# S5 output of a two-block layer: the chunk products moved ahead of the scan, into two open PSUM banks

## The chip, the cores and the metric

The kernel runs on one core of a Trainium2 chip. The metric is the time of one execution in device microseconds; less is better. Before the change it is 1471.91 us (median of three runs, 1470.84 to 1474.93).

## What is computed

The program computes two blocks of a model on 512 tokens of 1024 columns. The first block mixes the tokens by an S5 layer (256 columns) and an SSD layer (768 columns), then adds cross attention and a convolved feed-forward part. The second block has HGRN2 and forgetting attention and a mixture of 16 experts. The change lies in the S5 layer of the first block:

```python
bu_re = jnp.einsum('blgc,gpc->blgp', uf, bb_re)
bu_im = jnp.einsum('blgc,gpc->blgp', uf, bb_im)
...
_, _, h_re, h_im = lax.associative_scan(combine, (a_re, a_im, bu_re, bu_im), axis=1)
y = (jnp.einsum('blgp,gcp->blgc', h_re, c_re.astype(f32))
     - jnp.einsum('blgp,gcp->blgc', h_im, c_im.astype(f32)))
y = y + uf * d_skip.astype(f32).reshape(S5_GROUPS, S5_GROUP_DIM)
y = jax.nn.gelu(y.reshape(bsz, l, S5_WIDTH))
y = y * jax.nn.sigmoid(y @ w_glu.astype(f32))
```

There are 16 groups of 16 columns, each with 64 complex states.

## The kernel before

The kernel cuts the 512 tokens into 64 chunks of 8. Within a chunk the output is a plain matrix product of the chunk's inputs with a Toeplitz block (`s5T`, 128x128 for a group); what comes from earlier chunks is the product of the state before the chunk (`H`, 64 rows for a group, real and imaginary plane) with `s5O`. So the output of a group is one **chunk product** (128 rows, 64 moving columns) plus two **state products** (64 rows, 64 moving columns). Groups come in pairs `gp` of 8; of a pair, the group `g2 = 0` has its states in partitions 0 to 63, and `g2 = 1` in partitions 64 to 127.

`s5_main` (L661 to L765) does the S5 layer in order: the inputs `U` come from DRAM; 32 small products give the chunks' sums `S` (L686), which ScalarE takes from two PSUM banks to SBUF (L688); VectorE scans over chunks (L698 to L713) and forms the state before each chunk, first its real plane, then its imaginary one (L727 to L731); TensorE makes the output (L740 and L742); ScalarE takes it from PSUM (L744, `s_yo`); it goes through DRAM to change its layout (L745, L749), and then come the skip and the GELU (L754, L755), the gate's product (L760), its sigmoid (L762) and the result (L763). All products of this function are in full float32: for each the trace shows two weight loads and two matmuls, so counts in the trace are twice those in the code.

`s5_main` is a generator. It is put on a list of background work (L1048) and advanced a step at a time while the units of the projections are traced: first the projection to the SSD inputs x (128x512 tiles, L1026 to L1036), then that to z (128x260 tiles, L1055). Each unit of a projection is a row of matmuls L276, L277, L278 (three float32r products of a high and a low part) on weights that ScalarE (L270) and VectorE (L271) have split. After z follow the norm of the memory (`mem_norm`; L311, L334, L323, L315), the SSD layer and the projections of the memory to keys and values.

What stands where on each engine is then set by a scheduler: it puts the traced instructions into one in-order queue for each engine, by priority and by when it thinks that their operands are there. PSUM has 8 banks: 4 in the pool `pmm` (`mm`, projections), 2 in `ptr` (`tr`, transposes) and 2 in `psm` (`sm`), which S5 uses. Weights come on the queue of SyncE (SP), into slots that are freed by the splits.

Before the change the output loop opens a bank for `g2 = 0`, makes for each pair the chunk product and the two state products into 64 of its columns, evicts the bank and writes it out, and then does the same for `g2 = 1`:

```python
o = ps[:, gp * 64:gp * 64 + 64]
nc.tensor.matmul(o, s.s5T[:, g].rearrange("p c t -> p (c t)"), U[:, g], start=True, stop=False)
for i in range(2):
    nc.tensor.matmul(o, s.s5O[rows, i, gp].rearrange("p c t -> p (c t)"), H[rows, i, gp],
                     start=False, stop=i == 1)
```

The scheduler draws the first chunk product of each bank far ahead, behind L686.

Of the kernel before, what the change touches and what calls it, by code (L numbers as in the profile page):

```python
# [7 lines left out]
F32 = mybir.dt.float32  # L8
# [10 lines left out]
P = 128  # L19
T = 512  # L20
# [3 lines left out]
SLOT = 4 * 260    # values of a block of weights in a partition  # L24
# [7 lines left out]
CAP = 96          # slots of an expert in one go  # L32
# [8 lines left out]
class Split:  # L41
    """an operand as two float32r parts whose sum is the float32 value"""
# [5 lines left out]
class Back:  # L48
    """pieces of work traced between the units of a projection"""
# [21 lines left out]
class Kern:  # L71
# [11 lines left out]
    @contextmanager  # L83
    def ahead(s, n=3000):
        """what is traced here goes before what is ready with it"""
        tc = s.tc
        p = tc.cur_priority
        tc.cur_priority = p - n
        yield
        tc.cur_priority += n  # L90

# [1 line left out]
    def consts(s):  # L93
# [14 lines left out]
        # -1e30 where the free index is below the partition, and where it is above it  # L108
# [10 lines left out]
    def bcast_pe(s, pool, row, name):  # L119
        """a row of 1024 in all partitions"""  # L120
        t = pool.tile([P, D], F32, name=name)
        for half in range(2):
            cs = slice(half * 512, half * 512 + 512)
            ps = s.pmm.tile([P, 512], F32, name="mm")
            s.nc.tensor.matmul(ps, s.ones[0:1, :], row[:, cs], start=True, stop=True)
            s.nc.scalar.activation(t[:, cs], ps, AF.Copy)
        return t

# [1 line left out]
    def plan_units(s):  # L130
        """blocks of weights in the order in which they are used"""
# [59 lines left out]
        s.plan = []       # engines and fences of the next splits, where not the usual ones  # L191

    def ring(s, kind, of=None):
        """the pools of a ring, one slot of each in turn"""
# [4 lines left out]
    def fill(s, splits=999, most=999):  # L199
        """loads and splits ahead of their use, as far as the slots go"""  # L200
        nr, nh = len(s.rings["raw"]), len(s.rings["hi"])
        while True:
            if s.u_load < len(s.units) and s.raw_live < nr and most:
# [4 lines left out]
                if n == "w_in" and off % ld == 776:   # the last of z, then dt  # L208
# [27 lines left out]
    def wunit(s, n, off, ld, kk, cols, keep=0):  # L236
        """the next block; the blocks taken before the last keep ones are done with"""
# [18 lines left out]
    def later(s, f, k=0):  # L256
        """f is traced when the next block of weights is taken (k: so many later)"""
# [23 lines left out]
    def rstd(s, ss, n, width, pool, v0=None, out=None):  # L281
        """(ss / width + eps) ** -0.5 for [128, n], the power refined by a Newton step;
        v0 in place of eps"""
# [33 lines left out]
    def transposes(s, src, k0, nk, dst, tt, dk=None):  # L317
        """src [128, nk*128] of token tile tt to the k-tiles of dst"""
# [11 lines left out]
    def norm_T(s, x, gain, dst, tt):  # L330
        """rows x [128, 1024] of token tile tt, normalised, scaled; returned: transposed into dst"""
# [15 lines left out]
    def projT(s, src, cols, ld, hT, evac, halves=False):  # L347
        """256 columns from each of cols of src as [column, token] tiles: evac(i, psum)"""
# [29 lines left out]
    def projR(s, src, ld, nk, get, x, after, tail=3, mid=None, lag=2, order=None):  # L378
        """x[:, tt] += (rows of get(k)) @ src, 1024 columns; after(tt) when a token tile is complete:
        it returns what is left to do lag tiles later; mid(tt) when its first half is"""  # L380
# [32 lines left out]
    def softplus_neg(s, pool, ax, shape):  # L413
        """log1p(exp(-|x|)) from |x|"""
# [23 lines left out]
    def s5_params(s, pc, po):  # L438
        """per (pair of groups, state) on partitions: kernels of a chunk of 8 tokens.
        pc: parameter columns pool (short lived), po: results"""  # L440
        nc, A = s.nc, s.A
        V = nc.vector
        cm = s.cols1          # [128, 96] columns
# [30 lines left out]
        # cos and sin of th: whole turns taken off exactly, then the sine in [-pi, pi]  # L474
# [20 lines left out]
        # powers 0..8 of a: [128, re/im, power, gp]  # L495
# [7 lines left out]
        def cpow(dst, src, n1):  # L503
            """dst[n1+1 .. 2 n1] = src[n1] * src[1 .. n1]"""
# [13 lines left out]
        # powers of a^8: [128, re/im, power, gp], negated imaginary part as third plane  # L518
# [7 lines left out]
        # powers 7..0 of a: [re/im, gp, s]  # L526
# [4 lines left out]
        # f = (a - 1) / lambda  # L531
# [17 lines left out]
        # Bb = f * B: [128, re/im, gp, c]  # L549
# [11 lines left out]
        # O = C a^t, t = 0..7, its imaginary part negated: [128, re/im, gp, t, c]  # L561
# [20 lines left out]
        # Bb with each channel 8 times: [128, re/im, gp, (c, s)]  # L582
# [4 lines left out]
        # K[(c', s), g, (t, c)] = Re sum_p C a^t Bb, the same for each s  # L587
# [15 lines left out]
        # shift by s: Toeplitz blocks  # L603
# [11 lines left out]
        # X = a^(7-s) Bb, transposed to [(c, s), re/im, gp, (g2, p)]  # L615
# [25 lines left out]
        # O a: [128, re/im, gp, (c, t)]  # L641
# [6 lines left out]
        # re' = re ar - im ai, -im' = (-im) ar - re ai  # L648
# [12 lines left out]
    def s5_main(s, pe, pu, dr):  # L661
        """u -> gelu, gate; tokens as in s5ud, (token in a chunk, chunk)"""
# [19 lines left out]
        for i in range(2):  # L682
# [6 lines left out]
            yield  # L689
        p8 = s.p8  # L690
# [13 lines left out]
        # what enters each block of 8 chunks  # L704
# [11 lines left out]
        # state before each chunk  # L716
# [16 lines left out]
        yd = dr.tile([256, 512], F32, name="s5_yd")  # L733
        for g2 in range(2):
            rows = slice(g2 * 64, g2 * 64 + 64)
            ps = s.psm.tile([P, 512], F32, name="sm")
            for gp in range(8):
                g = 2 * gp + g2
                o = ps[:, gp * 64:gp * 64 + 64]
                nc.tensor.matmul(o, s.s5T[:, g].rearrange("p c t -> p (c t)"), U[:, g], start=True, stop=False)  # L740
                for i in range(2):
                    nc.tensor.matmul(o, s.s5O[rows, i, gp].rearrange("p c t -> p (c t)"), H[rows, i, gp],  # L742
                                     start=False, stop=i == 1)
            nc.scalar.activation(yo[:, g2].rearrange("p g c -> p (g c)"), ps, AF.Copy)  # L744
            nc.sync.dma_start(dap(yd, g2 * 8192, [[64, P], [16384, 8], [1, 64]]), yo[:, g2])  # L745
            yield
# [21 lines left out]
    def ssd_dt(s, pd, x):  # L768
        """from dt before its softplus, [token, (chunk, head)]"""
# [24 lines left out]
        ex = pd.tile([P, 3, 4, 12], F32, name="ssd_ex")   # exp of: cumulated, total, what is left  # L794
# [5 lines left out]
        # the cumulated values as rows (chunk, head), which a matrix product spreads over the partitions  # L800
# [22 lines left out]
    def ssd_mask_unit(s, pl, c, g):  # L823
        """(C B^T masked with the decay), transposed: [s, head, t]"""
# [17 lines left out]
    def ssd_main(s, pl, zs, mixT):  # L842
        """chunks of 128 tokens; zs: silu(z) in [token, channel]"""
# [3 lines left out]
        for c in range(4):  # L847
# [59 lines left out]
            # gate, norm, transposed  # L907
# [8 lines left out]
    def rows_T(s, pool, specs, name):  # L916
        """rows of 128 values, as columns"""
# [12 lines left out]
    def mixer1(s):  # L930
# [9 lines left out]
        with ExitStack() as xc:  # L940
# [14 lines left out]
            # the table of Square is loaded while x comes  # L955
# [23 lines left out]
        # the last third of z, and dt  # L979
# [11 lines left out]
        # u  # L991
        s.s5T = po.tile([P, 16, 16, 8], F32, name="s5_T")      # rows (c', s), columns (c, t)
# [14 lines left out]
        # B, C, x with their convolution  # L1007
# [42 lines left out]
        # z  # L1050
# [1269 lines left out]
```

## Time and profile before

| | us |
|---|---|
| median of three runs | 1471.91 |
| lowest, highest run | 1470.84, 1474.93 |
| span of the profiled execution, first to last instruction | 1470.4 |
| TensorE matmuls busy | 1418.8 (96%) |
| TensorE weight loads busy | 1146.5 (78%) |
| VectorE busy | 977.9 (67%) |
| ScalarE busy | 776.2 (53%) |
| mean granted TensorE clock | 0.978 of full speed |

The profile gives the span of the profiled execution; it is 0.4 us under the lowest run and 1.5 us under the median. TensorE is busy nearly all the time, and its granted clock is below full speed in a few stretches only. A busy share counts an instruction from its start to its end, so a TensorE that is busy can still be slow: at half its clock, or waiting between small products.

### The profile page before, as it was taken

To read this page: it belongs to the slowest core of one execution; us is meant where nothing else is said; L and a number is where in the kernel's file an instruction comes from. 1 tells how busy PE (TensorE), PEld (TensorE's weight loads), DVE (VectorE), ACT (ScalarE), POOL (GpSimd) and SP (SyncE) were. 2 spreads that over 40 slices of the span, in tenths; PEclk is the share of its full clock that TensorE was granted. 3 is DMA by queue.
4 is the path that set the end of the run, shared out by engine and by line. 5 is a ranking of instruction groups with operands and counts; after the bars stand their busy time and mean duration, and the time that the engine had idled before them with its cause. 6 is when DMAs were issued, how large, how long until landed. Compare 5 with 4: busy or idle time off the path is not lost. (4 is left out here: it accounts for less than half of the span.)

```text
span 1470.4 us, 20178 instructions
## 1 busy us (share of the span) xinstructions
PE 1418.8 (96%) x7467; PEld 1146.5 (78%) x7467; DVE 977.9 (67%) x1772; ACT 776.2 (53%) x1198; POOL 103.8 (7%) x103
## 2 busy tenths in 40 slices
PE   7999999999999999999999999999999599999996
PEld 6887988778788888888888889877887367777774
DVE  5989267665546444434463897676545599999997
ACT  6465264434424333323352696454433388888885
POOL 1000000010000000000000400000101211111111
PEclk9999699999999999999999999999999699999998
DMA  6353223423123333233222423130663899999993
GB/s 191 100 131 116 69 86 101 158 72 101 58 72 101 105 98 99 87 99 101 92 95 86 132 74 101 30 89 30 207 237 137 246 351 363 356 344 347 342 350 127
DMA packets 145934, 223.51 MB, mean 152 GB/s; under 512 B 18467, under 2 KB 71107, under 8 KB 145817
## 3 DMA queue, kind: packets, MB, share of 16 engines
q1 hardware_dynamic: 136852, 200.48, 41.8%
q0 software_dynamic: 3568, 10.34, 2.9%
q10 hardware_dynamic: 5412, 11.37, 2.2%
q8 instruction: 59, 0.97, 0.3%
q14 instruction: 43, 0.34, 0.1%
HBM read 208.41 MB, written 14.95 MB: 152 GB/s over the span
## 5 line engine op out<-in xcount | busy, mean ns | idle before, releaser
L271 DVE TENSOR_TENSOR wlo<-raw,whi 128x1024 fp32r<-128x1024 f32 (+1 forms) x351 | 423.5, 1221 | 236.9 <-ACT whi L270 234.4
L270 ACT ACTIVATE whi<-raw 128x1024 fp32r<-128x1024 f32 (+1 forms) x356 | 372.8, 1057 | 293.1 <-PE mm L277 143.1
L276 PE MATMUL mm<-hT_hi,whi 128*128 128x512 f32 (+1 forms) x768 | 283.3, 369 | 1.9 <-DVE x L403 1.7
L278 PE MATMUL mm<-hT_hi,wlo 128*128 128x512 f32 (+1 forms) x768 | 281.6, 367 | 0.0
L277 PE MATMUL mm<-hT_lo,whi 128*128 128x512 f32 (+1 forms) x768 | 280.8, 366 | 0.0
L276 PE MATMUL mm<-whi,hT_hi 128*128 128x512 f32 (+1 forms) x592 | 220.5, 373 | 1.8 <-ACT hT_hi L315 1.8
L278 PE MATMUL mm<-whi,hT_lo 128*128 128x512 f32 (+1 forms) x592 | 220.2, 372 | 0.0
L277 PE MATMUL mm<-wlo,hT_hi 128*128 128x512 f32 (+1 forms) x592 | 219.0, 370 | 0.0
L278 PEld LDWEIGHTS mm<-hT_hi,wlo 128*128 128x128 f32 x768 | 144.7, 188 | 24.4
L276 PEld LDWEIGHTS mm<-hT_hi,whi 128*128 128x128 f32 x768 | 144.2, 188 | 24.7 <-DVE x L403 1.9
L277 PEld LDWEIGHTS mm<-hT_lo,whi 128*128 128x128 f32 x768 | 144.6, 188 | 23.3
L276 PEld LDWEIGHTS mm<-whi,hT_hi 128*128 128x128 f32 x592 | 113.7, 192 | 20.7 <-ACT hT_hi L315 2.7
L278 PEld LDWEIGHTS mm<-whi,hT_lo 128*128 128x128 f32 x592 | 113.8, 192 | 19.6 <-issue 0.8
L277 PEld LDWEIGHTS mm<-wlo,hT_hi 128*128 128x128 f32 x592 | 113.9, 192 | 18.1 <-issue 0.6
L276 PE MATMUL mm<-whi,ex_xh 128*96 128x512 f32 x256 | 102.8, 402 | 1.3 <-ACT ex_xh L315 0.7
L291 POOL TENSOR_TENSOR rs_r<-rs_v,mhalf 128x1 f32<-128x1 f32 (+2 forms) x42 | 33.3, 797 | 998.8 <-DVE rs_v L289 842.7
L277 PE MATMUL mm<-wlo,ex_xh 128*96 128x512 f32 x256 | 101.5, 397 | 0.0
L278 PE MATMUL mm<-whi,ex_xl 128*96 128x512 f32 x256 | 101.1, 396 | 0.0
L276 PEld LDWEIGHTS mm<-whi,ex_xh 128*96 128x96 f32 x256 | 41.7, 163 | 19.1 <-ACT ex_xh L315 1.2
L278 PEld LDWEIGHTS mm<-whi,ex_xl 128*96 128x96 f32 x256 | 41.6, 162 | 18.0
L277 PEld LDWEIGHTS mm<-wlo,ex_xh 128*96 128x96 f32 x256 | 41.8, 163 | 17.0
L1238 DVE SCALAR_TENSOR_TENSOR cv<-mm,cols,cv 128x511 f32<-128x511 f32 (+1 forms) x44 | 33.0, 749 | 30.0 <-ACT cv L1235 29.2
(568 smaller groups left out, 2087.0 us busy)
## 6 DMA issues: line engine op xcount, KB each, us to landing
raw<-in_w_gate SPq DMA_DIRECT2D x64, 512.0 KB
raw<-in_w_up SPq DMA_DIRECT2D x64, 512.0 KB
raw<-in_w_down SPq DMA_DIRECT2D x64, 512.0 KB
raw<-in_ffn_w_up SPq DMA_DIRECT2D x44, 512.0 KB
raw<-in_w_in SPq DMA_DIRECT2D x40, 512.0 KB
raw<-in_ffn_w_down SPq DMA_DIRECT2D x22, 512.0 KB
raw<-in_w_out SPq DMA_DIRECT2D x16, 512.0 KB
raw<-in_w_in SPq DMA_DIRECT2D x8, 520.0 KB
```

Of the source, the lines that this page charges most:

```text
L270: s.hi_op = s.nc.scalar.activation(hv, v, AF.Copy).ins
L271: eng.tensor_sub(lv, v, hv.bitcast(F32))
L276: mm(ps, a.hi[asl], b.hi[bsl], start=first, stop=False)
L277: mm(ps, a.hi[asl], b.lo[bsl], start=False, stop=False)
L278: mm(ps, a.lo[asl], b.hi[bsl], start=False, stop=last)
L291: s.pow_op = nc.gpsimd.tensor_tensor(r, v, s.mhalf[:, :n], OP.pow).ins
L1238: V.scalar_tensor_tensor(y[:, d:], ps[:, :512 - d], cw[:, w:w + 1], y[:, d:], op0=OP.mult, op1=OP.add)
```

## The change

The sixteen chunk products move ahead of the scan: they are made as soon as `U` is there and ScalarE has emptied the two banks of L686, and both banks stay open with their sums until the end. A bank is started once (`start=gp == 0`); the other columns of a bank are then written for the first time without a start. Behind the scan only the 32 state products are left, in the order pair, plane, half: each is followed by one of the other row half, into the other bank. The two evictions and the two writes to DRAM stand together at the end.

```diff
             nc.scalar.activation(S[:, i].rearrange("p g c -> p (g c)"), ps, AF.Copy)
             yield
+
+        yps = [s.psm.tile([P, 512], F32, name="sm") for _ in range(2)]
+        for gp in range(8):
+            for g2 in range(2):
+                g = 2 * gp + g2
+                nc.tensor.matmul(yps[g2][:, gp * 64:gp * 64 + 64], s.s5T[:, g].rearrange("p c t -> p (c t)"), U[:, g],
+                                 start=gp == 0, stop=False)
+            if gp == 3:
+                yield
+        yield
         p8 = s.p8
...
         yd = dr.tile([256, 512], F32, name="s5_yd")
+
+        for gp in range(8):
+            for i in range(2):
+                for g2 in range(2):
+                    rows = slice(g2 * 64, g2 * 64 + 64)
+                    nc.tensor.matmul(yps[g2][:, gp * 64:gp * 64 + 64], s.s5O[rows, i, gp].rearrange("p c t -> p (c t)"),
+                                     H[rows, i, gp], start=False, stop=gp == 7 and i == 1)
         for g2 in range(2):
-            rows = slice(g2 * 64, g2 * 64 + 64)
-            ps = s.psm.tile([P, 512], F32, name="sm")
-            for gp in range(8):
-                g = 2 * gp + g2
-                o = ps[:, gp * 64:gp * 64 + 64]
-                nc.tensor.matmul(o, s.s5T[:, g].rearrange("p c t -> p (c t)"), U[:, g], start=True, stop=False)
-                for i in range(2):
-                    nc.tensor.matmul(o, s.s5O[rows, i, gp].rearrange("p c t -> p (c t)"), H[rows, i, gp],
-                                     start=False, stop=i == 1)
-            nc.scalar.activation(yo[:, g2].rearrange("p g c -> p (g c)"), ps, AF.Copy)
+            nc.scalar.activation(yo[:, g2].rearrange("p g c -> p (g c)"), yps[g2], AF.Copy)
             nc.sync.dma_start(dap(yd, g2 * 8192, [[64, P], [16384, 8], [1, 64]]), yo[:, g2])
-            yield
+        yield
```

The rest of the diff takes comments out. In the changed kernel the chunk products are L695, the state products L749, the evictions L752, the GELU L763 and the sigmoid L770; lines behind them are 8 higher than before.

How the scheduler then orders the engines is seen at three places. The names are tiles: `s_U`, `s_T`, `s_H`, `s_O` are U, s5T, H and s5O, `sm` a bank of `psm`.

TensorE behind the products L686, before:

```order
L686 MATMUL sm<-s_U,s_I 64x64 x32
L740 MATMUL sm<-s_U,s_T 128x64
L276 MATMUL mm<-hT_hi,whi 128x512
L277 MATMUL mm<-hT_lo,whi 128x512
L278 MATMUL mm<-hT_hi,wlo 128x512
```

and with the change:

```order
L686 MATMUL sm<-s_U,s_I 64x64 x32
L695 MATMUL sm<-s_U,s_T 128x64 x8
L276 MATMUL mm<-hT_hi,whi 128x512
L277 MATMUL mm<-hT_lo,whi 128x512
L278 MATMUL mm<-hT_hi,wlo 128x512
L276 MATMUL mm<-hT_hi,whi 128x512
L277 MATMUL mm<-hT_lo,whi 128x512
L695 MATMUL sm<-s_U,s_T 128x64 x8
```

All eight chunk products of the first bank now stand where one stood, and those of the second bank five projection matmuls later (its single one stood nine later before): 14 products are added here.

TensorE in the output, with the numbers of the buffers (before, the banks are sm_1451 and sm_1522), where the first bank ends and the second goes on:

```order
L740 MATMUL sm_1451<-s5_U_1152,s5_T_396 128x64
L742 MATMUL sm_1451<-s5_H_1146,s5_O_397 128x64 x2
L742 MATMUL sm_1522<-s5_H_1146,s5_O_397 128x64
L740 MATMUL sm_1522<-s5_U_1152,s5_T_396 128x64
L742 MATMUL sm_1522<-s5_H_1146,s5_O_397 128x64 x2
```

and with the change (banks sm_1225 and sm_1226), around the eight transposes of the memory's first tile:

```order
L749 MATMUL sm_1225<-s5_H_1146,s5_O_397 128x64
L749 MATMUL sm_1226<-s5_H_1146,s5_O_397 128x64
L749 MATMUL sm_1225<-s5_H_1146,s5_O_397 128x64
L323 MATMUL tr_1881<-ident_60,h_1867 128x128 x4
L323 MATMUL tr_1888<-ident_60,h_1867 128x128 x4
L749 MATMUL sm_1226<-s5_H_1146,s5_O_397 128x64
L749 MATMUL sm_1225<-s5_H_1146,s5_O_397 128x64
```

No product of 128 rows stands between the state products any more; 13 stand ahead of the transposes and 17 behind them, and the two halves take turns throughout. The first two state products, which need only the real plane, stand 14 projection matmuls earlier than before, with 14 projection matmuls between them and the rest (15 before); behind the last one come 57 projection matmuls up to the transposes of the memory's second tile.

ScalarE behind the memory's evictions, before:

```order
L315 ACTIVATE memT_hi<-tr 128x4x128 x4
L1055 ACTIVATE zs<-mm 128x260
L755 ACT_TABLE_LOAD
L755 ACTIVATE s_yg<-s_yg 128x512 x2
L1055 ACT_TABLE_LOAD
L1055 ACTIVATE zs<-mm 128x260
L762 ACT_TABLE_LOAD
L762 ACTIVATE s_sg<-sm 128x512
```

and with the change:

```order
L315 ACTIVATE memT_hi<-tr 128x4x128 x4
L763 ACT_TABLE_LOAD
L763 ACTIVATE s_yg<-s_yg 128x512
L1063 ACT_TABLE_LOAD
L1063 ACTIVATE zs<-mm 128x260
L763 ACT_TABLE_LOAD
L763 ACTIVATE s_yg<-s_yg 128x512
L1063 ACT_TABLE_LOAD
L1063 ACTIVATE zs<-mm 128x260
L770 ACT_TABLE_LOAD
L770 ACTIVATE s_sg<-sm 128x512
```

The two GELUs no longer stand together: an eviction of z stands between them, with two more table loads.

## Rows read from the trace of the kernel before

**Rows 1.** The page, 40 slices of the span: the TensorE clock granted, tenths.
```profile
PEclk9999699999999999999999999999999699999998
```

**Rows 2.** Windows: busy us of each engine (instructions), then granted clock, DMA share, GB/s.
```profile
core 0: us, PE busy (x) PEld busy (x) DVE busy (x) ACT busy (x) POOL busy (x), PEclk, DMA share, GB/s
112.00:145.00 33.00, 31.96 (x188) 27.40 (x186) 32.35 (x104) 17.18 (x27) 0.00 (x0) 1.00 0.41 129
145.00:147.00 2.00, 0.17 (x3) 0.05 (x2) 2.00 (x6) 0.00 (x0) 0.61 (x1) 1.00 0.00 0
147.00:150.50 3.50, 3.50 (x19) 3.36 (x19) 3.50 (x7) 1.06 (x1) 0.32 (x1) 0.58 0.00 0
150.50:154.00 3.50, 3.50 (x22) 2.88 (x20) 2.78 (x7) 1.15 (x2) 0.56 (x1) 0.93 0.30 79
155.50:162.00 6.50, 6.50 (x28) 5.56 (x27) 0.00 (x0) 0.00 (x0) 0.00 (x0) 0.50 0.00 2
178.30:184.00 5.70, 5.70 (x50) 5.70 (x50) 2.84 (x5) 3.53 (x7) 0.00 (x0) 1.00 0.52 183
...
200.00:220.00 20.00, 19.82 (x142) 17.03 (x142) 14.71 (x24) 10.95 (x25) 0.55 (x1) 1.00 0.35 111
```

**Rows 3.** Groups by line in 150.5 to 173.6 us, TensorE: busy us, mean ns | idle.
```profile
L742 PE MATMUL sm<-s_H,s_O 64*128 64x64 f32 x60 | 14.8, 401 | 0.0
L740 PE MATMUL sm<-s_U,s_T 128*128 128x64 f32 x28 | 8.7, 410 | 0.0
```

**Rows 4.** Timeline, TensorE before and behind the first state products: start us, us, instruction.
```profile
142.79 0.28 PE L278 MATMUL mm<-whi,hT_lo 128*128 128x260 f32 x1
...
144.84 0.28 PE L277 MATMUL mm<-wlo,hT_hi 128*128 128x260 f32 x1
146.95 0.44 PE L742 MATMUL sm<-s_H,s_O 64*128 64x64 f32 x4 [1.83 <-DVE rs_h L298]
...
148.79 0.42 PE L276 MATMUL mm<-whi,hT_hi 128*128 128x260 f32 x1
149.01 0.42 PE L277 MATMUL mm<-wlo,hT_hi 128*128 128x260 f32 x1
```

**Rows 5.** Timeline, VectorE: the last step of each plane of the state.
```profile
146.27 0.62 DVE L731 TENSOR_TENSOR s_H<-s_H,s_S 128x448 f32<-128x448 f32 x1
...
148.74 0.63 DVE L731 TENSOR_TENSOR s_H<-s_H,s_S 128x448 f32<-128x448 f32 x1
```

**Rows 6.** Timeline, weight loads of the first two state products, one of each half.
```profile
146.95 0.30 PEld L742 LDWEIGHTS sm<-s_H,s_O 64*128 64x128 f32 x4 [2.04 <-DVE s_H L731]
```

**Rows 7.** Timeline, TensorE in the output, early and at its end.
```profile
151.17 0.43 PE L740 MATMUL sm<-s_U,s_T 128*128 128x64 f32 x2
...
152.12 0.43 PE L740 MATMUL sm<-s_U,s_T 128*128 128x64 f32 x2
...
171.89 0.69 PE L740 MATMUL sm<-s_U,s_T 128*128 128x64 f32 x2
...
173.55 0.58 PE L278 MATMUL mm<-whi,hT_lo 128*128 128x260 f32 x1
```

**Rows 8.** Timeline, TensorE: products in runs, L686 of S5 and L871 of SSD.
```profile
106.35 2.08 PE L686 MATMUL sm<-s_U,s_I 128*64 128x64 f32 x64
...
204.97 0.78 PE L871 MATMUL sm<-ssd_xdt,ssd_L 128*128 128x64 f32 x6
205.58 0.33 PE L832 MATMUL sm<-neg_lt,identb 128*128 128x384 bf16 x1
```

**Rows 9.** Timeline, TensorE: transposes of the memory's second tile.
```profile
181.18 0.60 PE L323 MATMUL tr<-ident,h 128*128 128x128 f32 x4
181.53 0.37 PE L278 MATMUL mm<-whi,hT_lo 128*128 128x260 f32 x1
```

**Rows 10.** Timeline, ScalarE: the table load ahead of the GELU.
```profile
183.27 1.28 ACT L755 ACT_TABLE_LOAD   x1
```

**Rows 11.** Waits in 150 to 260 us: who waited for whom, us in total, times, longest.
```profile
ACT whi L270 <- DMA raw<-in_xa_wk: 0.3, 1, 0.3
```

## The prediction

> **What bounds the kernel now.** I read the clock's slices of the page first [rows 1]: full speed nearly everywhere, with a drop in the slice from 147 to 184 us, where the S5 output lies. Then the windows around it [rows 2]. Up to 145 us TensorE is busy 31.96 of 33.00 us at the full clock (2.4 GHz), and VectorE 32.35: the scan keeps VectorE as full as TensorE. From 145 to 147 TensorE does almost nothing; it waits 1.83 us for the state's first plane [rows 4], which VectorE ends at 146.89 [rows 5]. Behind this idle time the clock is at 0.58 on the mean, and in the output from 155.5 at 0.50, the lower level (1.2 GHz). It is full again in the window from 178.3. VectorE and ScalarE stand at 0.00 busy in the middle of it: nothing else sets the pace, TensorE alone does, and its busy time here is made of slow small products.
>
> How slow: of the output, 60 state matmuls and 28 chunk matmuls lie in 150.5 to 173.6 [rows 3] (a product is two matmuls). One chunk product and two state products, six matmuls, take 152.12 - 151.17 = 0.95 us at the full clock and 173.55 - 171.89 = 1.66 us at the lower one [rows 7]. Six matmuls of the chunk product's own shape in a run, L871 of the SSD layer, take 205.58 - 204.97 = 0.61 us, 0.102 each [rows 8]. So the mixture costs 0.34 us a group over a run of one shape at the full clock. Each group goes once from 128 rows to 64 and once back: I put it on that, 0.17 us a switch, and at the lower clock (1.66 - 2 x 0.61) / 2 = 0.22.
>
> **The change part by part.** I count from the first state products to a fixed point, the transposes of the memory's second tile, at 181.18 [rows 9]; TensorE's queue does the same work up to there in both kernels, apart from the output itself.
>
> *Chunk products, 28 matmuls added at 108 to 112 us.* The trace has them only singly there; the nearest row is the run of L871 at 0.102: 2.9 us. Bounds: 0.0325 each, as L686 runs (2.08 / 64 [rows 8], half as many weight columns, two column halves in turn), is 0.9 us; 0.95 / 6 = 0.16 each, as in the mixture, is 4.4 us. I take 2.9, since the shape is that of L871. It delays everything behind it on TensorE, but 14 projection matmuls move from before the first state products to behind them. One takes 0.12 us (17 steps from 142.79 to 144.84, 2.05 us [rows 4]), so 1.7 us. TensorE would have come to the state products at 145.1 (146.95 less the idle 1.83); now at 145.1 + 2.9 - 1.7 = 146.3, still ahead of VectorE's 146.89. The delay goes into the existing wait. That cover is thin: VectorE has 0.65 us of idle time in 112 to 145 [rows 2], and its convolutions get their inputs from TensorE up to 2.9 us later, with scan steps drawn ahead of them. I let 0.5 us pass on: first state products at 147.4 (bounds 146.9, nothing passes, and 149.8, all 2.9).
>
> *State products.* The price of a run in which the halves alternate is seen in small: the first two, one of each half, stand together in the kernel before. Their four weight loads take 0.30 us altogether at 0.19 each [rows 6], which is two side by side and the next two 0.11 us later; the four matmuls span 0.44 [rows 4]. So 0.11 us for a pair, one matmul of each half: 0.056 each. Bounds: 0.051 (half of 0.102, both halves wholly at once) and 0.102 (no overlap). I take 0.056, from the very instruction: 60 matmuls, 3.4 us (3.1 to 6.1).
>
> Here a rule speaks against the change. By the Trainium skill, TensorEngine Tiling (Array Packing), Instruction Overhead, a matmul carries a fixed overhead of some 60 cycles, and a tiling factor should not be taken where a dimension is already small; with 64 moving columns that would make the halves' overlap worth little, and the sum would be with 0.102, 2.7 us longer than mine. The weight loads of this case lie side by side all the same, 0.30 us for four, so I go by the row.
>
> *The sum from 147.4 on.* First two state products 0.4 (their four matmuls span 0.44 [rows 4]). 14 projection matmuls: the idle time ahead of them stays (about 1.8 us, since VectorE still comes last), and behind it the trace had the lower clock, 149.01 - 148.79 = 0.22 each [rows 4]: 3.0 (1.7 if the clock stays). The imaginary plane is then long there (149.37 before [rows 5], 0.5 later now): 0.3 for what waits remain. State products 3.4. Eight transposes at 0.35 for four [rows 9]: 0.7. 57 projection matmuls at 0.12: 6.8. Together 14.6, so the fixed point is at 162.0 instead of 181.2: **19.2 us earlier**.
>
> Of the 19.2, 28 chunk matmuls and their switches are the smaller part; the rest is the state products in a run, and the clock, which stays up when the matmuls follow each other at the pace of 200 to 220 us, where runs of L871 lie in a stretch at 1.00 [rows 2].
>
> *Behind the fixed point.* ScalarE loads two more tables of 1.28 us [rows 10] between the GELUs and evictions of z; TensorE has other matmuls queued, but the gate's products and free banks for z wait for ScalarE's queue. Bounds 0 and 2.6; I take 1.0, as ScalarE has a good third of its time free there (3.53 of 5.70 busy [rows 2]). The two evictions stand together, so the first write to DRAM is later by one bank, but both before anything that now needs them. On SP one weight load moves behind the reads of this result; its slot is needed for the keys' projection, some 30 us later: nothing. From there the queues pace each other as before, and I let the gain run to the end.
>
> Sum: 2.9 is in the start at 147.4; 19.2 - 1.0 = 18.2 us. The profiled span is 1470.4, so 1452.2; the median is 1.5 over that span: **1453.7**, rounded to 1454.
>
> **The rivals.**
>
> *The clock stays low through the output,* as it did before from 155.5 on [rows 2]. For: it fell in a stretch that looked busy too, and the idle time ahead stays. Against: the matmuls now follow each other three times as densely (0.056 against 0.16). At the lower clock, from 147.4: 0.4 + 3.0 + 0.3 + 6.8 + 1.4, then some 20 projection matmuls at 0.22 and 37 at 0.12, 8.8: 20.7, the fixed point at 168.1, a gain of 13.1 - 1.0 = 12.1: 1460. If the halves don't overlap either, 12.2 in place of 6.8, gain 6.7: 1465.
>
> *The gain is given back to a weight wait.* All of TensorE's work up to the keys comes 18 us sooner; if the weights for the keys don't, it stops there. For: the split of these weights waited 0.3 us for its transfer already [rows 11]. Against: the transfers are started by slots that the splits free, so they come sooner too, and DMA share is 0.00 in 155.5 to 162 [rows 2]. Where a load were fixed in time, up to all 18 us: 1470 to 1472.
>
> *Slower: the products don't follow each other.* Alternating between halves and banks may make each state product wait until the one before has left the array. A state matmul lasts 401 ns from start to end [rows 3], so a product of two would cost 0.8 us unpipelined at the lower clock, 30 of them 24 us in place of 3.4, with the rest at the lower clock as above: the fixed point at 147.4 + 0.4 + 3.0 + 0.3 + 24.0 + 1.4 + 8.8 = 185.3, 4.1 us later than before, and with 1.0 behind it 1477. It decides from about 0.66 us a product (no gain). Against: L686 alternates too and runs at 0.0325 a matmul [rows 8].
>
> **How the numbers follow.** Forecast 0.65 (its own range 1450 to 1458: a clock that never falls takes off 1.3, no loss on ScalarE 1.0, a loss of 2.6 and a passed-on delay of 2.9 add 4). Low clock 0.24. Given back 0.06. Not running in turn 0.03. The remaining 0.02 I count as no change. A measurement of this kernel tells about 0.3%, 4.4 us, from no change. Faster by more: forecast and low clock and half of the given-back case, 0.92. Same 0.05, slower 0.03. The range reaches from the forecast's lower end into the low-clock case: 1450 to 1464.
>
> **What would show it.** In the profile after: 32 matmuls L695 in two runs of some 1.6 us at 108 to 112 us; the first L749 at about 147.4 behind a wait for VectorE; the 60 others within 3 to 4 us around the transposes, with a clock near 1.00; the memory's second transposes near 162. A last L749 later than 160, or a granted clock at 0.50 beyond 155, is the first rival. A fixed point near 162 with a total above 1460 would mean that a later stage takes the gain back, and I would be wrong on that it runs to the end.

## The result, and the profile after

| | before | changed |
|---|---|---|
| median of four runs each, us | 1473.06 | 1455.49 |
| lowest, highest | 1470.84, 1474.93 | 1453.98, 1456.92 |
| span of the profiled execution | 1470.4 | 1452.2 |
| mean granted clock | 0.978 | 0.987 |

The ratio is 0.9881, with a 95% interval of 0.9863 to 0.9899: 17.6 us faster between the medians, 18.2 between the profiled executions. The forecast was 1454, in 1450 to 1464. (The kernel before has a fourth run here, 1474.20, beside the three whose median was 1471.91.)

The clock of the page no longer falls in the slice from 145 to 182 us, where [rows 1] had a 6:

```profile
PEclk9999999999999999999999999999999699999998
```

Windows from the state to the end of the output in the changed kernel, beside [rows 2] (busy us of PE, PEld, DVE, ACT, POOL, then granted clock, DMA share, GB/s):

```profile
147.00:150.50 3.50, 3.03 (x30) 2.75 (x32) 3.43 (x9) 0.39 (x1) 1.00 (x1) 1.00 0.02 5
150.50:155.50 5.00, 5.00 (x67) 4.69 (x66) 2.84 (x6) 2.09 (x4) 0.55 (x1) 1.00 0.00 0
155.50:162.00 6.50, 6.31 (x53) 6.10 (x51) 3.09 (x4) 3.90 (x7) 0.00 (x0) 1.00 0.90 232
```

The clock is 1.00 in all of them; before it was 0.58 behind the wait and 0.50 in the output. TensorE's timeline shows the steps of the prediction (start, us, instruction; most projection matmuls are left out):

```profile
107.97 2.00 PE L695 MATMUL sm<-s_U,s_T 128*128 128x64 f32 x16
109.78 0.48 PE L276 MATMUL mm<-hT_hi,whi 128*128 128x512 f32 x1
...
111.02 1.89 PE L695 MATMUL sm<-s_U,s_T 128*128 128x64 f32 x16
112.73 0.48 PE L278 MATMUL mm<-hT_hi,wlo 128*128 128x512 f32 x1
...
147.36 0.44 PE L749 MATMUL sm<-s_H,s_O 64*128 64x64 f32 x4 [1.47 <-DVE s_H L741]
...
149.78 1.77 PE L749 MATMUL sm<-s_H,s_O 64*128 64x64 f32 x26
151.52 1.06 PE L323 MATMUL tr<-ident,h 128*128 128x128 f32 x8
152.51 2.22 PE L749 MATMUL sm<-s_H,s_O 64*128 64x64 f32 x34
154.66 0.39 PE L278 MATMUL mm<-whi,hT_lo 128*128 128x260 f32 x1
...
162.19 0.63 PE L323 MATMUL tr<-ident,h 128*128 128x128 f32 x4 [0.38 <-DVE memT_lo L315]
```

The 60 state matmuls take 1.74 + 2.15 us around the transposes, and the fixed point of the prediction is at 162.19 in place of 181.18 [rows 9]. TensorE's waits from 100 to 285 us (engine, line <- who it waited for: us in total, times, longest) hold no weight load, and ScalarE once, at a transpose ahead of the output that waited 1.0 us in the kernel before:

```profile
PE sm L749 <- DVE s_H L741: 1.5, 1, 1.5
PE tr L1043 <- ACT xt L1026: 0.7, 1, 0.7
...
PE tr L323 <- DVE memT_lo L315: 0.4, 1, 0.4
```

To compare kernels I take the stretch from the start of L686 to the first addition to the residual behind the S5 and SSD layers, L403 on VectorE. All kernels do the same other work in it. In the kernel before, and in the changed one:

```profile
106.35 2.08 PE L686 MATMUL sm<-s_U,s_I 128*64 128x64 f32 x64
298.09 1.28 DVE L403 TENSOR_TENSOR x<-x,mm 128x512 f32<-128x512 f32 x2
```

```profile
105.95 2.09 PE L686 MATMUL sm<-s_U,s_I 128*64 128x64 f32 x64
279.61 1.28 DVE L403 TENSOR_TENSOR x<-x,mm 128x512 f32<-128x512 f32 x2
```

So 191.74 and 173.66: **the stretch is 18.08 us shorter**. The changed kernel also reaches L686 0.40 us sooner, where the two do the same work (the start varies from 105.78 to 108.08 over all the profiles), and 0.28 is lost behind L403: 18.2 in all. Executions of one kernel differ by up to 10 us with the mean granted clock (the kernel before, beside the last experiments: 1468.5 us at 0.982 to 1478.5 at 0.975), so parts of a few us are read from this stretch in the profiled executions, and the medians stand beside it. The changed kernel profiled twice gives 173.66 and 173.55 (e11). Each ratio is to runs of the kernel before made beside that experiment.

### The profile page after: what moved, and what is told of

The parts are those of the page before. It is cut to its first block, busy times and chain, and to the rows that moved or that the text cites. A ratio compares the mean times of both kernels' runs of the same rounds, so it can differ in the third digit from the quotient of the medians.

```text
span 1452.2 us, 20178 instructions
## 1 busy us (share of the span) xinstructions
PE 1399.7 (96%) x7467; PEld 1130.2 (78%) x7467; DVE 977.7 (67%) x1772; ACT 779.2 (54%) x1200; POOL 103.8 (7%) x103
## 4 chain that ended last, share of the span: by engine, by line
PE 86%; DVE 6%; ACT 3%; DMA 2%; issue 2%; POOL 1%; DVEq 0%; SPq 0%; ACTq 0%; POOLq 0%
PE mm L276 24%; PE mm L278 24%; PE mm L277 24%; PE sm L1416 2%; PE tr L1548 1%; PE tr L323 1%; PE tr L1887 1%; PE sm L1532 1%; POOL rs_r L291 1%; DMA ex_g<-xnd,sn_i 1%; DVE wlo L271 1%; PE sm L879 1%; PE sm L276 1%; PE tr L1540 1%; PE sm L2028 1%
```

## Experiments

| kernel | L686, L403 start | stretch | less the change's | median us | ratio to before, interval |
|---|---|---|---|---|---|
| change | 105.95, 279.61 | 173.66 | | 1455.49 | 0.9881 (0.9863 to 0.9899) |
| e1_chunks_behind | 106.14, 280.14 | 174.00 | +0.34 | 1456.82 | 0.9888 (0.9855 to 0.992) |
| e2_halves_apart | 106.14, 282.78 | 176.64 | +2.98 | 1461.07 | 0.9931 (0.9898 to 0.9964) |
| e3_mixed | 106.33, 282.88 | 176.55 | +2.89 | 1462.43 | 0.9928 (0.9907 to 0.9948) |
| e4_no_chunks | 106.23, 278.04 | 171.81 | -1.85 | 1456.04 | 0.9884 (0.9851 to 0.9916) |
| e5_before_filled | 107.77, 299.40 | 191.63 | +17.97 | 1473.69 | 0.9994 (0.9981 to 1.0006) |
| e6_one_gelu | 106.39, 279.71 | 173.32 | -0.34 | 1455.72 | 0.9865 (0.9848 to 0.9881) |
| e7_same_rows | 106.04, 283.67 | 177.63 | +3.97 | 1460.46 | 0.9904 (0.9888 to 0.9921) |
| e8_pool_plane | 106.41, 287.34 | 180.93 | +7.27 | 1462.72 | 0.9916 (0.99 to 0.9933) |
| e9_column_halves | 108.08, 281.23 | 173.15 | -0.51 | 1455.58 | 0.9872 (0.985 to 0.9893) |
| e10_ssd_halves | 105.78, 278.56 | 172.78 | -0.88 | 1456.20 | 0.9881 (0.9861 to 0.9901) |
| e11_change_again | 106.96, 280.51 | 173.55 | -0.11 | 1457.39 | 0.988 (0.986 to 0.99) |

My theory at the start: the gain is the order of the products (no changes of shape, halves in turn) and the clock that this order keeps up. The rivals: it is the place ahead of the scan; it is the wait ahead of the state that took the clock down.

**e1: the chunk products as a run at the end.**

```diff
-        for gp in range(8):
-            for g2 in range(2):
-                g = 2 * gp + g2
-                nc.tensor.matmul(yps[g2][:, gp * 64:gp * 64 + 64], s.s5T[:, g].rearrange("p c t -> p (c t)"), U[:, g],
-                                 start=gp == 0, stop=False)
-            if gp == 3:
-                yield
...
-                                     H[rows, i, gp], start=False, stop=gp == 7 and i == 1)
+                                     H[rows, i, gp], start=gp == 0 and i == 0, stop=False)
+        for gp in range(8):
+            for g2 in range(2):
+                g = 2 * gp + g2
+                nc.tensor.matmul(yps[g2][:, gp * 64:gp * 64 + 64], s.s5T[:, g].rearrange("p c t -> p (c t)"), U[:, g],
+                                 start=False, stop=gp == 7)
```

> The 16 chunk products stand as one run behind the 32 state products (halves alternating) instead of ahead of the scan. My theory (the order of the products has a price, and hiding the chunk products in the scan is the smaller part): 32 chunk matmuls at 0.10 to 0.11 are now 3.4 us behind the state products, and some 0.3 us of further waits; span 1455 to 1456.5 against 1452.2 of the change, clock full in the output. Rival 1 (hiding the chunk products is what brings the gain, the order is not): nearly all of the 18 us is lost again, 1467 to 1471. Rival 2 (the longer idle time ahead of the state takes the clock down, and the run does not hold it up): the output at 0.50, 1461 to 1464.

The timeline of TensorE:

```profile
146.83 0.44 PE L743 MATMUL sm<-s_H,s_O 64*128 64x64 f32 x4 [1.94 <-DVE s_H L735]
150.01 1.06 PE L323 MATMUL tr<-ident,h 128*128 128x128 f32 x8
151.01 3.57 PE L743 MATMUL sm<-s_H,s_O 64*128 64x64 f32 x60
154.50 3.79 PE L748 MATMUL sm<-s_U,s_T 128*128 128x64 f32 x32
```

and its window behind the wait:

```profile
147.00:150.50 3.50, 3.35 (x29) 3.10 (x30) 3.50 (x6) 2.38 (x4) 0.00 (x0) 1.00 0.00 0
```

Rival 1 falls: next to nothing of the gain is lost with the products behind the scan. But I was wrong as well: not 3.4 us, 0.34. TensorE has work to do on either side of the scan, and the chunk products take the same 3.5 us wherever they stand; moving them ahead only pushes other matmuls behind. What counts is how long TensorE waits for the state: 1.94 us here, 1.47 in the change, 1.83 before [rows 4]. **The place that names the change is worth 0.3 us** with the clock up in both. Rival 2 falls in this execution too: the clock was 1.00 through the wait and the output. (e4 below shows that it can fall behind the same wait.)

**e2: one half after the other; e7: the order of the change, but the same rows for both halves.**

```diff
-        for gp in range(8):
-            for i in range(2):
-                for g2 in range(2):
+        for g2 in range(2):
+            for gp in range(8):
+                for i in range(2):
```

> As the change, but all state products of the first row half (and bank) before all of the second. My theory (products of two halves lie side by side in the array): without a neighbour of the other half each matmul takes 0.10 to 0.11 us instead of 0.056, 56 to 60 of them 2.5 to 3.4 us more; span 1454.7 to 1455.6, clock full. Rival 1 (what the change removed is only the alternation of 128 and 64 rows; the halves do not matter): 0.056 each here too, 1452.2. Rival 2 (at half the density the clock falls): 6 us and more in the output's two parts, up to 1459.

```diff
-                    rows = slice(g2 * 64, g2 * 64 + 64)
+                    rows = slice(0, 64)
```

> As the change, order and banks the same, but the state products of the second half take the first half's rows (so half of the groups get the state of another group). My theory (two row halves work side by side): all products now want the same rows, each matmul takes 0.10 to 0.11 us instead of 0.056, 60 of them 2.8 to 3.4 us more, 1455.0 to 1455.6. Rival (the two banks in turn bring it, not the halves): 0.056 each, 1452.2.

The first stretch of state matmuls in the timeline of e2, and of e7, and a window of e7 behind its last state matmul:

```profile
149.95 3.11 PE L749 MATMUL sm<-s_H,s_O 64*128 64x64 f32 x26
152.99 1.09 PE L323 MATMUL tr<-ident,h 128*128 128x128 f32 x8
```

```profile
149.89 3.11 PE L749 MATMUL sm<-s_H,s_O 64*128 64x64 f32 x26
152.93 1.09 PE L323 MATMUL tr<-ident,h 128*128 128x128 f32 x8
```

```profile
157.00:162.00 5.00, 5.00 (x30) 4.88 (x30) 1.23 (x1) 2.53 (x5) 0.00 (x0) 0.66 0.53 127
```

26 matmuls take 3.04 us (152.99 - 149.95, 152.93 - 149.89) in place of 1.74: 0.117 with the changes of shape at both ends, against 0.067. In e7 the banks still take turns, so **it is the two row halves, not the two banks,** and it is worth 3.0 us. What e7 loses beyond this is the clock: 0.66 in 157 to 162 us. The clock of e2 is 1.00 from 112 to 220 us in the profiled execution; its median is 5.6 us above the change's, and its other executions have mean clocks of 0.978 to 0.983, so its rival 2 may have come there, where no trace shows it. Whether two halves could take turns in one bank was not tried.

**e3: the mixture, in groups of two chunk and four state products.** The loop that e1 takes out of its place stands here inside the output loop:

```diff
+            for g2 in range(2):
+                g = 2 * gp + g2
+                nc.tensor.matmul(yps[g2][:, gp * 64:gp * 64 + 64], s.s5T[:, g].rearrange("p c t -> p (c t)"), U[:, g],
+                                 start=gp == 0, stop=False)
             for i in range(2):
```

> Chunk products again inside the output loop, but in groups: two chunk products, then four state products of halves in turn, eight times. My theory (0.17 us for a switch between 128 and 64 rows, 0.107 for a chunk matmul, 0.056 for a state matmul): 28 x 0.107 + 60 x 0.056 + 15 x 0.17 = 8.9 us for what takes 3.4 in the change: with a full clock 1457.7. Rival 1 (the mixture takes the clock down, however it is grouped): twice that, and the matmuls behind it until the clock is back, 1466 to 1469. Rival 2 (switches are free, and only the density counts): 28 x 0.107 + 3.4 = 6.4, 1455.2.

```profile
154.42 0.66 PE L742 MATMUL sm<-s_U,s_T 128*128 128x64 f32 x4
...
155.60 0.66 PE L742 MATMUL sm<-s_U,s_T 128*128 128x64 f32 x4
```

(TensorE's timeline.) A group takes 155.60 - 154.42 = 1.18 us at full clock. In runs it would be 4 x 0.112 + 8 x 0.056 = 0.90 (0.112 is a state matmul of e7 with no neighbour, and a chunk matmul of the change, 1.81 us for 16), so a change of shape costs 0.14, not 0.17. Against rival 2, the changes are not free. My number missed by 2.6 (5.5 forecast over the change, 2.89 measured), mainly for the reason of e1: I counted the chunk products as added (28 x 0.107 = 3.0), and they are only moved. In this execution the clock was 0.60 behind the wait of 1.82 us, as before, and then full in nearly all of the mixture, against rival 1 (windows):

```profile
147.00:150.50 3.50, 3.50 (x19) 3.26 (x19) 3.50 (x7) 1.06 (x1) 0.32 (x1) 0.60 0.00 0
...
155.50:162.00 6.50, 6.50 (x66) 5.89 (x65) 0.00 (x0) 1.58 (x4) 0.00 (x0) 1.00 0.19 58
```

The median, 3.5 us above this execution, and its mean clocks of 0.979 to 0.983 say that in others it was not; where, no trace shows.

**e4: the chunk products left out.** The edit is e1's without the loop at the end.

> As the change, but the chunk products are left out (the output lacks the part of each chunk's own inputs). My theory (the 3.5 us of chunk products ahead of the scan lie in time in which TensorE waits for VectorE anyway): the wait ahead of the state grows to 2.5 us and more, the first state product comes 0.3 to 0.5 us sooner, span 1451.7. Rival 1 (the chunk products cost their time): 3.5 us off, 1448.7. Rival 2 (an idle time of over 1.8 us takes the clock down): some stretch behind the wait at 0.50, 1453 to 1456.

My theory falls: the wait did not grow to 2.5 us. It is 1.92, as in e1 (timeline). Both rivals show: the stretch is 1.85 us shorter, and the clock fell behind the wait, which it did not in the change (windows):

```profile
146.94 0.44 PE L743 MATMUL sm<-s_H,s_O 64*128 64x64 f32 x4 [1.92 <-DVE s_H L735]
...
147.00:150.50 3.50, 3.50 (x22) 3.43 (x23) 3.50 (x7) 1.61 (x3) 0.00 (x0) 0.69 0.00 0
150.50:155.50 5.00, 5.00 (x68) 4.83 (x68) 4.17 (x8) 1.82 (x3) 0.56 (x1) 0.88 0.47 141
```

Up to the wait e4 and e1 do the same. In e1 the transposes stand at 150.01 and the state products behind them at 151.01; here at 151.01 and 152.33, 1.3 us later by the clock alone. With it the chunk products' price is 1.85 + 1.3, about 3.2 of their 3.5 us: rival 1 held on the price. The median, 1456.04, shows nothing of it, at mean clocks of 0.983 and 0.984 in the other three executions.

**e5: the wait ahead of the old output, filled.** The kernel that ran has 12 of the products, not the 18 that the expectation names.

```diff
             ps = s.psm.tile([P, 512], F32, name="sm")
+            if g2 == 0:
+                for _ in range(12):
+                    nc.tensor.matmul(ps[:, 0:128], s.ident, c.rearrange("p i g a -> p (i g a)"), start=True, stop=True)
```

> The kernel before, with 18 products (128x128, float32, on the carries) put into the first bank of the output ahead of the first chunk product; they are overwritten, and fill the time in which TensorE waited for the state. My theory (the mixture itself lets the clock fall, not the wait ahead of it): no fall in or right behind the wait, then half clock in the mixture as before; 6 records of it again 0.95 us at first and 1.66 later; span 1468 to 1472. Rival (the wait lets the clock fall, and the mixture only keeps it down): full clock throughout, 15 groups of 0.95 = 14.3 us for the mixture instead of 22.9, and the matmuls behind the wait at 0.12: 1459 to 1461.

The windows, and TensorE's timeline in the output:

```profile
147.00:150.50 3.50, 2.69 (x23) 2.41 (x22) 3.50 (x8) 0.00 (x0) 0.93 (x1) 1.00 0.00 0
150.50:155.50 5.00, 4.86 (x35) 4.11 (x33) 3.27 (x7) 1.54 (x3) 0.56 (x1) 1.00 0.01 3
155.50:162.00 6.50, 6.50 (x28) 5.56 (x27) 0.00 (x0) 0.00 (x0) 0.00 (x0) 0.53 0.19 61
```

```profile
153.72 0.43 PE L743 MATMUL sm<-s_U,s_T 128*128 128x64 f32 x2
...
154.67 0.43 PE L743 MATMUL sm<-s_U,s_T 128*128 128x64 f32 x2
...
157.09 0.69 PE L743 MATMUL sm<-s_U,s_T 128*128 128x64 f32 x2
...
158.75 0.47 PE L743 MATMUL sm<-s_U,s_T 128*128 128x64 f32 x1
```

With the wait cut to 0.81 us there is no fall behind it, and the clock falls all the same, at 155.5, when the mixture has run for 3 us: groups of 0.95 us become groups of 1.66. The ten runs all lie within 1472.6 to 1474.2. **The clock falls in the mixture itself**; a fall behind the wait, or a wait as long as the old one, is not needed for it. That holds for groups of one chunk and two state products: in e3's execution, with groups twice as long, it did not fall. The other way to settle it, the mixture with no wait at all, was not tried.

**e6: one GELU over both halves.**

```diff
-            nc.scalar.activation(yg[:, m], yg[:, m], AF.Gelu_apprx_tanh)
+        nc.scalar.activation(yg.rearrange("p m n -> p (m n)"), yg.rearrange("p m n -> p (m n)"), AF.Gelu_apprx_tanh)
```

> As the change, but one GELU over both halves, so that no eviction of z stands between and two table loads of 1.28 us go. My prediction gave the loads a price of 1.0 us: span 1451.2. Rival (TensorE waits for nothing of ScalarE in 164 to 174 us of the changed kernel, so the loads lie beside its work): within 0.4 us of the change, 1451.8 to 1452.5.

The stretch is 0.34 shorter: the rival. (The span is 1454.7, with a fall of the clock near 808 us that the changed kernel's first profile does not have.) All but 0.3 us of the two loads lies beside TensorE's work.

**e8: the imaginary plane on GpSimd.**

```diff
-            V.tensor_mul(Hv[:, i], cb(i), pb(0))
-            V.tensor_mul(hv, cb(1 - i), pb(2 if i == 0 else 1))
+            E = nc.gpsimd if i else V
+            hi = hv2 if i else hv
+            E.tensor_mul(Hv[:, i], cb(i), pb(0))
+            E.tensor_mul(hi, cb(1 - i), pb(2 if i == 0 else 1))
...
```

> As the change, but the imaginary plane of the state is formed on GpSimd while VectorE forms the real one, and the state products go plane by plane. My theory (VectorE, which ends the planes one after the other, sets the start of the output): the real plane 1.2 us sooner, the imaginary one 1 us sooner (four steps of 1.3 us on GpSimd from 142.7), TensorE's idle time 1.0 instead of 1.86: span 1451.2 to 1451.8. Rival (GpSimd's steps are slower on these shapes, or slow VectorE beside them): the imaginary plane after 150, span 1452.5 to 1456.

The timeline of GpSimd, VectorE and TensorE, and the window of the output:

```profile
143.25 2.47 POOL L741 TENSOR_TENSOR s_H<-s_cy,s_p 128x512 f32<-128x512 f32 x1 [40.50 <-DVE s_cy L723]
145.67 2.20 POOL L742 TENSOR_TENSOR s_ht<-s_cy,s_p 128x512 f32<-128x512 f32 x1
...
143.19 1.20 DVE L741 TENSOR_TENSOR s_H<-s_cy,s_p 128x512 f32<-128x512 f32 x1
144.31 2.37 DVE L742 TENSOR_TENSOR s_ht<-s_cy,s_p 128x512 f32<-128x512 f32 x1
...
150.07 3.25 PE L753 MATMUL sm<-s_H,s_O 64*128 64x64 f32 x28 [4.17 <-DVE s_H L745]
```

```profile
150.50:155.50 5.00, 5.00 (x49) 4.88 (x48) 2.06 (x6) 1.15 (x2) 1.61 (x3) 0.50 0.02 3
```

The rival, and more than its price: GpSimd's first step takes 2.47 us, not 1.3 (a product of the same size takes 1.30 there in L2210 of the change), and VectorE's second one 2.37 where the same step (L738) takes 1.12 to 1.20 in the change. TensorE waits 4.17 us, and the clock is 0.50 in the output, although the halves take turns. The Trainium skill (SBUF — State Buffer, SBUF: two separate sides) says that a VectorE operation with two inputs in SBUF and a GpSimd operation take one shared pair of ports in turn, each for its whole length; the trace agrees: VectorE's first step, begun just before GpSimd's, keeps its 1.20 us, and the three that begin during a step of the other engine grow by 0.9 to 1.2, about what is left of that step.

**e9, e10: column halves** (both with the GELU of e6), and **e11: the change again.**

```diff
+                for r in (0, 64):
+                    nc.tensor.matmul(yps[g2][r:r + 64, gp * 64:gp * 64 + 64],
+                                     s.s5T[:, g].rearrange("p c t -> p (c t)")[:, r:r + 64], U[:, g],
+                                     start=gp == 0, stop=False)
...
```

> As the change, with each chunk product made as two of 64 output rows (column halves of the array in turn, as L686 does), and one GELU. The runs so far say that chunk products cost their time wherever they stand, and that a change of shape costs 0.14 us. My theory (column halves lie side by side like row halves): 64 matmuls at 0.0325 = 2.1 us in place of 3.5, less up to 0.3 for one more change of shape; counted from the first product L686 to a point behind the S5 layer 1.1 to 1.4 us less for this and 0.3 for the GELU: 1.4 to 1.7 us less than the change. Rival (128 rows by 64 columns cost the same in halves as whole): only the 0.3 of the GELU.

> As e9_column_halves, and the 48 products of the SSD layer with 64 moving columns (L879 of the change) in column halves too. Theory (it pays everywhere): 192 matmuls at 0.0325 = 6.2 us in place of 96 at 0.102 to 0.112, 3.6 to 4.5 us less than e9_column_halves. Rival, which I hold for likelier (a change of shape costs 0.14 us on each side, and these products stand in groups of three between products of full width): 16 groups of 12 x 0.0325 + 0.28 = 0.67 us, as much as a group of 6 x 0.102 to 0.112 = 0.61 to 0.67 takes now: within 1 us of e9_column_halves.

> The changed kernel itself, once more, beside the two others on one chip. As before: 1454 to 1457 us, 0.987 to 0.989 of the time of the kernel before; a granted clock of 1.00 from 112 to 200 us. Rival (the profiled execution was a lucky one): the clock falls in the output in this execution, and the median lies above 1457.

The chunk products of e9, in halves of 64 output rows, and TensorE's waits that grew:

```profile
110.00 1.10 PE L696 MATMUL sm<-s_U,s_T 128*64 128x64 f32 x32
111.03 0.50 PE L276 MATMUL mm<-hT_hi,whi 128*128 128x512 f32 x1
...
112.38 1.15 PE L696 MATMUL sm<-s_U,s_T 128*64 128x64 f32 x32 [0.17 <-ACT s_S L688]
113.47 0.50 PE L277 MATMUL mm<-hT_lo,whi 128*128 128x512 f32 x1
```

```profile
PE tr L1045 <- ACT xt L1028: 1.3, 2, 0.7
PE tr L323 <- DVE memT_lo L315: 0.6, 1, 0.6
PE tr L323 <- DVE h L334: 0.5, 1, 0.5
```

They take 1.03 + 1.09 = 2.1 us in place of 1.81 + 1.71 = 3.5, as the theory has it; but only 0.5 of the forecast 1.4 to 1.7 arrives at L403, 0.34 of it the GELU's. TensorE comes sooner to what ScalarE and VectorE end, and waits there: for ScalarE 1.3 us in place of 0.7, for VectorE ahead of the transposes 1.1 in place of 0.4. In e10 the SSD products in halves bring 0.37 more, nearer to the rival (no gain) than to the 3.6 of the theory. The medians of e9 and e10 cannot be told from the change's own beside them. e11 repeats the change: 173.55 in the stretch, ratio 0.988. Its median, 1457.39, is above the 1457 that I gave as the upper end, so half of the rival's sign came. The other half did not: its clock is full in the stretch, but 0.50 in 808 to 812 us, where the change's first profile had 1.00 (windows, first e11, then the change):

```profile
808.00:812.00 4.00, 3.84 (x18) 3.85 (x19) 3.26 (x14) 3.10 (x7) 1.07 (x2) 0.50 0.70 252
```

```profile
808.00:812.00 4.00, 3.55 (x31) 3.33 (x30) 3.32 (x9) 3.38 (x7) 0.87 (x2) 1.00 0.45 169
```

So the first profile was among the shorter executions, as its time, 1453.98, says: the lowest of the ten runs of this kernel.

## Why the prediction was right

It was right in its number and, in the main, in its steps: 18.2 us between the profiled executions were forecast and 18.2 measured. That the two agree to a tenth is luck: terms that were too small and too large by more than a microsecond cancel, and 0.40 of the lead stands ahead of the S5 layer, where the change does nothing.

- *First state products at 147.4*: 147.36, behind a wait of 1.47 us for VectorE. The 32 chunk matmuls take 3.5 us, 0.112 each inside the run and not the 0.102 of L871 [rows 8]; four took 0.4 there before, so 3.1 are added, for 2.9.
- *14 matmuls behind the wait at the low clock, 3.0*: wrong; the wait shrank from 1.83 to 1.47 us, where I had let it stay, the clock stayed up, and they took 1.8. The imaginary plane then ended the wait at 149.78, 1.3 us before my 151.1.
- *60 state matmuls in 3.4*: 1.74 + 2.15 = 3.9, with the changes of shape around the transposes that I did not count; inside the run a pair takes the forecast 0.11. Against this I had set the overhead of some 60 cycles a matmul (the Trainium skill, TensorEngine Tiling (Array Packing), Instruction Overhead). What I read out of it, that the overlap of halves is worth little at 64 columns, the traces do not bear out: without a neighbour 0.112, with one 0.056, 3.0 us in all (e2).
- *Transposes 0.7*: 1.0. *57 matmuls 6.8*: 7.15, and 0.38 of a new wait for the memory's first tile. The overruns, 1.5, nearly cancel with the 1.2 that the clock behind the wait gave, and the fixed point is at 162.19 for 162.0.
- *ScalarE 1.0*: 0.5. The lead is 18.99 at the fixed point, 0.40 of which the kernel had before the S5 layer (L686 at 105.95 against 106.35), and 18.08 at L403: 18.59 - 18.08. Of it 0.34 go with the GELU (e6); what the rest is, no run shows.
- *The gain runs to the end*: the lead is 18.48 at L403 (298.09 - 279.61) and 18.2 at the end; TensorE waits for no weights up to L403.
- *Median 1.5 over the span*: 3.3 (1455.49 - 1452.2). The time of the profiled execution itself, 1453.98, is 1.8 over its span, and the median is 1.5 over that, as executions such as e11's are longer. (Of the prediction's own range, 1450 to 1458, the terms named for its lower end, 1.3 and 1.0, give 1451.4.)

Where the 18.08 come from, as an estimate: 0.3 the place ahead of the scan (e1); 3.0 halves in turn (e2); 30 changes of shape at 0.14, 4.2. The rest, about 10.6, I put on the clock. Two other ways give about the same. From rows of the kernel before: the output from 155.5 to 173.55 at 0.95 / 1.66 of its length saves 7.7 [rows 7], the matmuls from there to 178.3 at 0.12 for 0.22 save 2.2, and 15 behind the wait at 0.12 for 0.22 save 1.5: 11.4, less the new wait of 0.38 and the 0.5 of ScalarE's step. And e3, with the clock full in nearly all of the output, is 15.2 us under the kernel before (191.74 - 176.55); less 3.0 for halves in turn and 2.1 for 15 changes of shape fewer, 10.1. So **well over half of the gain is the clock,** which I had named with the state products' run as one term. This share is worked out: no run has the old order with the clock full throughout. And the chunk products' place, which I had hidden in VectorE's wait, hides little: they push 14 matmuls behind the state, and the wait shrinks by 0.4.

The rivals: the low clock (chance 0.24) did not come in the changed kernel's two profiles, but e8 shows it with the halves in turn, plane by plane, after a wait of 4.17 us, and e7 behind matmuls without a neighbour. Given back, and not in turn: neither; no wait for weights, and pairs at 0.11 us.

## What to carry to other kernels

Small float32 products were cheapest here in runs of one shape with row halves, or column halves, in turn; each change of shape cost 0.14 us, and the thin mixture far more, as TensorE's clock fell in it. Where TensorE is busy on both sides of a wait, moving its work into the wait gains only what the wait gets shorter; look at the wait, not at the moved work. Leaving work out of TensorE need not show in the time, if the clock falls as well: without the chunk products the median is 1456.04 (e4), with them 1455.49.

## What was not expected of the hardware

- The clock behind a wait is not set by the wait's length alone: it stayed at 1.00 behind 1.94 us (e1) and fell behind 1.83 (before, 0.58), 1.82 (e3, 0.60) and 1.92 (e4, 0.69), though e1 and e4 do the same work up to there. Behind the shorter waits of the other kernels with the change's order of chunk products (1.36 to 1.47 us in the change, e2, e6, e7, e9, e10 and e11) it was 1.00 every time; so the 0.4 us by which the change shortens the wait may be part of why the clock stayed up, which no run tests by itself. The same stretch near 808 us had 1.00 in one execution of the changed kernel and 0.50 in another (e11). What decides it stays open.
- VectorE and GpSimd on the same kind of step slow each other to about double the time (2.37 us for 1.12 to 1.20, 2.47 for 1.30).
